# Low parts of split weights: an accumulating DMA in place of a vector subtraction, in a four-layer fp32 model

## The chip, the cores and the metric

One NeuronCore of a Trainium2 chip runs the whole program in one launch. The metric is the device time of one execution in microseconds (us), first instruction to last. Engines are named as the profile names them: PE (TensorE matmul), PEld (its weight loads), DVE (VectorE), ACT (ScalarE), POOL (GpSimd), SP (the sync engine, which only issues DMAs here). A small q behind a name (SPq) is the engine's own queue, where DMAs are issued.

## The reference, cut to what matters

Input x is 512 tokens by 1024 features, all in float32. Four mixing layers (L1: SSD and gated linear attention; L2: multi-head latent attention; L3: retention; L4: stick-breaking attention) each have a SwiGLU feed-forward layer behind them (F1 to F4, hidden width 2816):

```
for each layer:  x = x + mixer(rms_norm(x) * gain);  x = x + (silu(h @ w_gate) * (h @ w_up)) @ w_down
```

Nearly all of the arithmetic is products of activations with some 240 MB of weights, each weight used once per execution.

## The kernel before, in words

**Split operands.** Each float32 product is made of three passes on PE in the float32r type. An operand a is split into a high part (a rounded by a copy to float32r) and a low part (a minus the high part). A product is high·high + high·low + low·high, summed in PSUM: `mm3` (line 355) issues weights' high with the activations' high, weights' high with the activations' low, and weights' low with the activations' high. `mm3t` (line 454) does the same with the activations as the stationary operand; there the pass with the weights' low part is the second.

**Weight pieces.** The weights come in 455 pieces of at most 128 x 1024 float32 (512 KB), in the order of their use (`plan`, line 292). A piece passes through three steps. `wload` (line 330) has SP load it from DRAM to a tile `wr`. `wconv` (line 337) makes its high part `wh` with an ACT copy, and its low part `wl` with a DVE subtraction. `wpiece` (line 347) hands the two to the products. The tiles `wr`, `wh` and `wl` come from the pool `self.wp` with three buffers each, so a piece can be converted only when the piece three before it has had its last product. Helpers carry the line numbers of the profile: L221 is every ACT activation (`act`), L205 every two-operand vector operation (`tt`), L224 every matmul (`mm`), L334 the load of a piece.

```
def wconv(self):
    if self.raws:
        raw, ap = self.raws.popleft()
        n = ap.shape[-1]
        hi = self.wp.tile([128, 1024], F32R, tag="wh", name=self.nm("wh"))
        lo = self.wp.tile([128, 1024], F32R, tag="wl", name=self.nm("wl"))
        self.act(hi[:, :n], raw[:, :n], AF.Copy)
        self.tt(lo[:, :n], raw[:, :n], hi[:, :n].bitcast(F32), ALU.subtract)
        self.convs.append((hi, lo, ap))
...
def wpiece(self, ap):
    while len(self.convs) < 2 and self.raws:
        self.wconv()
        self.wload()
    hi, lo, at = self.convs.popleft()
```

**Who uses pieces.** Most pieces carry 8 stationary tiles of 128 x 128, used once each by `lin_a` (line 409) or `lin_b` (line 422): 24 passes a piece. In the feed-forward layers (`ffn`, line 471) 44 gate and up pieces are followed by 8 output tiles of the down projection, each of three pieces (1024, 1024 and 768 columns). `lin_bs` (line 436) differs: it takes all pieces of a block first, and then goes over the four token tiles, using each piece again in every one. In L2 (`mla`, line 930) a block of one 1024-column piece (keys and values) is followed by a block of two (768 and 384 columns, queries). In L4 (`sb`, line 1241) eight blocks have two 1024-column pieces each, so that two of the three buffers are in use for the whole block.

**Order.** The kernel is written as one sequence; the tile framework puts each engine's instructions in an order at compile time, from its own model of when each will be ready, and adds the semaphore waits. The order of an engine's instructions can so differ from the written one. In the mixing layers the steps of attention and of the scans run between the products as background work (`fill`, line 244, after each three-pass product). POOL has few instructions: sums of squares for the norms (L205), masks of layer 1 (L679), and some products. No DMA is issued from POOL. ACT reads PSUM and makes all exponentials, gates and high parts.

Of the kernel before, what the change touches and what calls it, by code (L numbers as in the profile page):

```python
# [9 lines left out]
F32 = mybir.dt.float32  # L10
# [7 lines left out]
EPS = 1e-6  # L18
# [148 lines left out]
class Emit:  # L167
# [15 lines left out]
        self.uid = 0  # L183
        self.ctx = ctx

# [1 line left out]
    def nm(self, s):  # L187
        self.uid += 1
        return f"{s}_{self.uid}"
# [52 lines left out]
        return True  # L242

    def fill(self):
        """called after each three-pass product: background steps at the set rate"""
        self.vn += 1
        if self.vq and self.vn % 2 == 0:
            self.vq.popleft()()
        if self.bg:
            self.credit += self.rate  # L250
            while self.credit >= 1.0:
                self.credit -= 1.0
                self.pump(1)
# [12 lines left out]
        self.pump(10 ** 9)  # L266

    def rsqrt(self, src, n, mul, out=None):
        """(src * mul + EPS) ** -0.5, elementwise on [128, n]"""
        v, i, a, y = self.S(n, "rv"), self.S(n, "ri", I32), self.S(n, "ra"), self.S(n, "ry")  # L270
        self.ts(v, src, mul, EPS, ALU.mult, ALU.add)
        self.ts(i, v.bitcast(I32), 1, None, ALU.logical_shift_right)
        self.ts(y.bitcast(I32), i, -1.0, float(0x5F3759DF), ALU.mult, ALU.add)
        for _ in range(3):
            self.stt(a, y, -0.5, y, ALU.mult, ALU.mult)
            self.mul(a, a, v)
            self.stt(y, a, 1.5, y, ALU.add, ALU.mult)
        return y

    def split(self, src, gain, name="h"):  # L280
        """src (SBUF or PSUM, times a per-partition gain) as float32r high and low parts"""
        n = src.shape[-1]
        hi, lo = self.T2(F32R, (128, n), name + "h"), self.T2(F32R, (128, n), name + "l")
        if gain is None:
            self.act(hi, src, AF.Copy)
            self.tt(lo, src, hi.bitcast(F32), ALU.subtract)
        else:
            self.act(hi, src, AF.Copy, scale=gain)
            self.stt(lo, src, gain, hi.bitcast(F32), ALU.mult, ALU.subtract)
        return hi, lo  # L290

    def plan(self, layers):
        """the weight pieces in the order of their use"""
        A = self.A
        for l in layers:
            if l[0] == "F":
                gu, wd = A[f"wgu{int(l[1]) - 1}"], A[f"wd{int(l[1]) - 1}"]
                for m in range(NFF):
                    yield gu[m, 0]
                    yield gu[m, 1]  # L300
                for m in range(8):
                    for c in (0, 1024, 2048):
                        yield wd[m][:, c:min(c + 1024, 2816)]
            elif l == "L1":
                yield from (A["w1a"][i] for i in range(12))
                yield from (A["w1b"][g, j] for g in range(2) for j in range(4))
                yield A["w1s"]
                yield from (A["w1a"][i] for i in range(12, 20))
                yield from (A["w1b"][g, j] for g in range(2, 6) for j in range(4))
                yield from (A["wo1"][i, m] for i in range(2) for m in range(8))  # L310
            elif l == "L2":
                yield from (A["wdq"][i] for i in (3, 4))
                yield A["wkr"]
                yield from (A["wdq"][i] for i in range(3))
                for g in range(4):
                    yield A["wukv"][g]
                    yield A["wuq"][g][:, 0:768]
                    yield A["wuq"][g][:, 768:1152]
                yield from (A["wo2"][i, m] for i in range(2) for m in range(4))
            elif l == "L3":  # L320
                for hd in range(4):
                    yield from (A["w3a"][4 * hd + i] for i in range(4))
                    yield from (A["w3b"][2 * hd + i, j] for i in range(2) for j in range(4))
                yield from (A["wo3"][i, m] for i in range(2) for m in range(8))
            elif l == "L4":
                yield from (A["w4b"][g, j] for g in range(2) for j in range(4))
                yield from (A["w4a"][g, s, j] for g in range(4) for s in range(2) for j in range(2))
                yield from (A["wo4"][i, m] for i in range(2) for m in range(4))
# [8 lines left out]
# [4 lines that stand above are left out]
            hi = self.wp.tile([128, 1024], F32R, tag="wh", name=self.nm("wh"))  # L341
            lo = self.wp.tile([128, 1024], F32R, tag="wl", name=self.nm("wl"))
            self.act(hi[:, :n], raw[:, :n], AF.Copy)
            self.tt(lo[:, :n], raw[:, :n], hi[:, :n].bitcast(F32), ALU.subtract)
            self.convs.append((hi, lo, ap))

    def wpiece(self, ap):
# [10 lines left out]
        self.mm(out, wl, xh, False, stop)  # L358
        self.fill()

# [1 line left out]
    def norm_prep(self, m, gain):  # L362
        self.h.append(self.split(self.x[:, m, :], self.col(gain, m)))
        self.norm_sq(m)
# [7 lines left out]
            self.add(self.acc, self.acc, sq, None if m == 7 else self.nc.gpsimd)  # L372

    def tok_sums(self, acc):
        """sums over the partitions of acc [128, 512], per token: [128 tok, 4]"""
        ps = self.MX()
        for t in range(4):
            self.mm(ps[:, t:t + 1], acc[:, t * 128:(t + 1) * 128], self.ones[:, 0:1])
        return ps

    def bcast_tok(self, r):
        """r [128 tok, 4] -> [128, 512], the tokens along the free axis on every partition"""
        ps = self.MX()
        for t in range(4):
            self.mm(ps[:, t * 128:(t + 1) * 128], r[:, t:t + 1].to_broadcast([128, 128]), self.ident)
# [2 lines left out]
        return o  # L388

    def norm_finish(self):  # L390
        """the row scales, rT and rbc, among the products that follow; row_scales() before their use"""
        def sums():
            ps = self.tok_sums(self.acc)
            self.rT = self.rsqrt(ps[:, 0:4], 4, 1.0 / 1024)
# [9 lines left out]
    def row_scales(self):  # L404
        if self.rbc is None:
            self.vflush()

# [1 line left out]
    def lin_a(self, pieces, hs, M=128):  # L409
        """pieces: [(ap [128, nk * M], nk)]; out [M, 512] features on partitions, in PSUM"""  # L410
        ps = self.LIN()
        K = sum(nk for _, nk in pieces)
        k = 0
# [6 lines left out]
        return ps  # L420

    def lin_b(self, pieces, hs, n=512):
        """pieces: [(ap [128, nk * n], nk)]; 4 x [128 tok, n] in PSUM"""
        pss = [self.LIN(), self.LIN(), self.LIN(), self.MX()]
        K = sum(nk for _, nk in pieces)
        k = 0
# [7 lines left out]
        return pss  # L434

    def lin_bs(self, pieces, hs, n):
        """as lin_b with the pieces all held: yields (t, [128 tok, n]) one after the other"""
        ws = []
        for ap, nk in pieces:
            wh, wl = self.wpiece(ap)  # L440
# [5 lines left out]
            yield t, ps  # L446

    def mm3s(self, out, w, x, n, start, stop):
        """a three-pass product of two split operands, n columns"""
        self.mm(out[:, 0:n], w[0], x[0][:, 0:n], start, False)  # L450
        self.mm(out[:, 0:n], w[0], x[1][:, 0:n], False, False)
        self.mm(out[:, 0:n], w[1], x[0][:, 0:n], False, stop)
# [14 lines left out]
                self.h = []  # L467
            self.norm_prep(m, gain)

# [1 line left out]
    def ffn(self, li, nxt):  # L471
        A = self.A
        self.norm_finish()
# [22 lines left out]
            self.residual(m, ps, gain)  # L496

    def out_two(self, w, hs, gain):
        """K = 512: a piece carries two output tiles"""
        for mp in range(4):  # L500
            wh, wl = self.wpiece(w[mp])
            for i in range(2):
# [3 lines left out]
                    self.mm3(ps, wh[:, s], wl[:, s], hs[k][0], hs[k][1], k == 0, k == 3)  # L506
                self.residual(2 * mp + i, ps, gain)

# [1 line left out]
    def ssd_gla(self, nxt):  # L510
        nc, A = self.nc, self.A
        self.norm_finish()
# [61 lines left out]
        self.out_a(A["wo1"][1], self.yh[8:16], nxt)  # L574

    def mix1(self):
        """the background steps of layer 1 in order"""
        def weave(main, side, at):
            n = 0
            for _ in main:  # L580
# [168 lines left out]
                yield  # L749

    def gla_gates(self):
        """cumulative log gates (times 16) of the four heads, restarting in each 64-token chunk"""
        nc = self.nc
        es, gs = [], []
        for hd in range(4):
# [106 lines left out]
            self.yh[8 + 2 * hd + i] = self.split(pt, self.col("glan", i))  # L862
            yield

# [1 line left out]
    def attention(self, nh, ready, prep, first, vcols, lag):  # L866
        """prep(hd): list of (lag, fn); first(hd, b): the weights of a 128-query block, st["p", b];
        vcols(hd, j): the values of the 128 keys of tile j, [128, 64]"""
        t, due, state = 0, [], {}
        todo = [(hd, b) for hd in range(nh) for b in range(4)]  # L870
        i = 0
# [31 lines left out]
            yield None if ran or due else "blocked"  # L903

    def weights_T(self, hd, j):
        """the weights of key tile j for the queries that see it, keys on partitions"""
        st = self.att[hd]
        pt = self.MX()
        for b in range(j, 4):
# [5 lines left out]
            self.act(wT[:, j * 128:], pt[:, j * 128:], AF.Copy)  # L915

    def pair_out(self, hp, vcols):
        """two heads' outputs, features on partitions, side by side in the array's columns"""
        po = self.MX()
        for j in range(4):  # L920
            for e in range(2):
# [4 lines left out]
            self.att.pop(2 * hp + e)  # L926
        self.oh[hp] = self.split(po, None)

# [1 line left out]
    def mla(self, nxt):  # L930
        nc, A = self.nc, self.A
        self.norm_finish()
# [22 lines left out]
        rk = self.rsqrt(self.tok_sums(acck)[:, 0:4], 4, 1.0 / 256)  # L955
        accq = down((0, 1, 2))
        cqh = [self.split(cf[i], self.col("qlora", i)) for i in range(3)]
        # rope tables with the gains in them, [128, 4, 32]
        self.ropec, self.ropes = self.S(128, "rc"), self.S(128, "rs")
        nc.sync.dma_start(out=self.ropec, in_=A["ropec"])  # L960
        nc.sync.dma_start(out=self.ropes, in_=A["ropes"])
# [42 lines left out]
                fn()  # L1004

    def mla_krope_a(self, kr):
        """the shared rotary part of the keys, under the heads' own parts in kT"""
        nc, tabs = self.nc, self.tabs
        pt = self.MX()
        for t in range(4):  # L1010
# [143 lines left out]
        hh, _, _, vs = self.heads[hd]  # L1154
        return vs[j][:, 64 * hh:64 * hh + 64]

# [1 line left out]
    def ret(self, nxt):  # L1158
        nc, A = self.nc, self.A
        self.norm_finish()  # L1160
# [76 lines left out]
            self.yh[4 * hd + i] = self.split(pt, self.col("retn", 4 * hd + i))  # L1237
            yield

# [1 line left out]
    def sb(self, nxt):  # L1241
        nc, A = self.nc, self.A
        self.norm_finish()
# [175 lines left out]
```

## Time and profile before

| | |
|---|---|
| time, two runs | 2818.6 and 2819.79 us, median 2819.19 |
| span of the profiled execution | 2818.6 us |
| PE, ACT, DVE, POOL busy | 99%, 36%, 52%, 5% of the span |
| DMA | 244.84 MB, 87 GB/s; SP's queue keeps the 16 DMA engines busy for 27.6% of the span |
| granted TensorE clock | 0.998 of 2.4 GHz over the span |

The span is the time from the first instruction to the last of one profiled execution, and the sums are made against it. A busy PE means that a matmul was in flight; matmuls overlap, so that a duration of 0.39 us and a start every 0.227 us go together. A row of the timeline gives the start in us, the duration in us, the engine, the line, the operation, its output and inputs, and in brackets the engine's idle time before it with what ended it.

### The profile page before, as it was taken

The numbers are of one execution on the slowest core, as the hardware profiler recorded it, in microseconds if no ns is written. First come the engines' busy times: TensorE is split into PE (matmuls) and PEld (weight loads), VectorE is DVE, ScalarE is ACT, GpSimd is POOL, SyncE is SP. The second block draws the span as 40 slices with busy tenths as digits, with TensorE's granted clock in tenths as the row PEclk, the third lists the DMA queues.
The fourth block names the chain that finished last, engine by engine and source line by source line (L and its number), as shares of the span: only waits on it lengthen the run. The fifth ranks groups of instructions, "written<-read, shape, count | busy, mean of one in ns | idle before, by whom it ended". The sixth has DMA issues, their size and how long they took to land.

```text
span 2818.6 us, 33289 instructions
## 1 busy us (share of the span) xinstructions
PE 2792.1 (99%) x13205; PEld 2259.5 (80%) x13205; DVE 1458.1 (52%) x2412; ACT 1020.0 (36%) x1629; POOL 152.2 (5%) x134
## 2 busy tenths in 40 slices
PE   8999999999998999999999999999999999999999
PEld 6787668888876678888888888888888987788887
DVE  7476564444349964443345554544433488744432
ACT  5444333332236652222233332332322365533321
POOL 1011001000012110000000000100000100100000
PEclk9999999999999999999999999999999999999999
DMA  4232212323321112333332222223333211133232
GB/s 155 85 106 93 72 53 92 98 95 98 96 78 40 46 60 97 97 97 90 115 96 85 77 87 82 90 97 98 96 96 97 87 53 45 53 96 98 93 105 80
DMA packets 72698, 244.84 MB, mean 87 GB/s; under 512 B 8208, under 2 KB 10064, under 8 KB 72544
## 3 DMA queue, kind: packets, MB, share of 16 engines
q1 hardware_dynamic: 72544, 242.72, 27.6%
q8 instruction: 104, 1.70, 0.2%
q14 instruction: 50, 0.41, 0.0%
HBM read 240.56 MB, written 2.13 MB: 86 GB/s over the span
## 4 chain that ended last, share of the span: by engine, by line
PE 94%; DVE 2%; issue 2%; ACT 1%; POOL 0%; DMA 0%; SPq 0%; POOLq 0%; ACTq 0%; DVEq 0%
PE lin L224 80%; PE mx L224 11%; PE mx L228 2%; POOL sq L205 0%; DVE wl L205 0%; DVE hl L214 0%; ACT wh L221 0%; DVE y L205 0%; ACT sq L221 0%; ACT hh L221 0%; DMA L<-acd 0%; DVE m L1143 0%; DVE e L769 0%; DMA x<-in_xT_dram 0%; DVE x L205 0%
## 5 line engine op out<-in xcount | busy, mean ns | idle before, releaser
L221 ACT ACTIVATE wh<-wr 128x1024 fp32r<-128x1024 f32 (+1 forms) x455 | 471.3, 1036 | 1279.5 <-PE lin L224 666.9
L224 PE MATMUL lin<-hh,wh 128*128 128x512 f32 (+1 forms) x2136 | 841.3, 394 | 7.6 <-ACT wh L221 7.5
L224 PE MATMUL lin<-hl,wh 128*128 128x512 f32 (+1 forms) x2136 | 835.9, 391 | 0.7 <-DVE hl L214 0.6
L224 PE MATMUL lin<-hh,wl 128*128 128x512 f32 (+1 forms) x2136 | 834.7, 391 | 0.8 <-DVE wl L205 0.8
L205 DVE TENSOR_TENSOR wl<-wr,wh 128x1024 fp32r<-128x1024 f32 (+1 forms) x455 | 545.7, 1200 | 477.6 <-ACT wh L221 477.1
L224 PEld LDWEIGHTS lin<-hh,wh 128*128 128x128 f32 (+1 forms) x2136 | 401.1, 188 | 98.3 <-issue 7.8
L224 PEld LDWEIGHTS lin<-hl,wh 128*128 128x128 f32 (+1 forms) x2136 | 401.4, 188 | 86.7 <-DVE hl L214 3.6
L224 PEld LDWEIGHTS lin<-hh,wl 128*128 128x128 f32 (+1 forms) x2136 | 401.1, 188 | 86.6 <-DVE wl L205 2.0
L224 PE MATMUL lin<-fh,wh 128*128 128x512 f32 x704 | 273.9, 389 | 0.0
L224 PE MATMUL lin<-fl,wh 128*128 128x512 f32 x704 | 273.9, 389 | 0.0
L224 PE MATMUL lin<-fh,wl 128*128 128x512 f32 x704 | 273.9, 389 | 0.0
L224 PE MATMUL lin<-wh,hh 128*128 128x512 f32 (+2 forms) x720 | 261.3, 363 | 0.8 <-ACT v L221 0.7
L224 PE MATMUL lin<-wh,hl 128*128 128x512 f32 (+2 forms) x720 | 252.3, 350 | 0.0
L224 PE MATMUL lin<-wl,hh 128*128 128x512 f32 (+2 forms) x720 | 251.7, 350 | 0.0
L205 DVE TENSOR_TENSOR u<-lin,bc 128x512 f32<-128x512 f32 x88 | 60.8, 691 | 282.5 <-PE lin L224 282.5
L205 POOL TENSOR_TENSOR sq<-sq,sq 128x512 f32<-128x512 f32 x51 | 76.1, 1492 | 1704.3 <-ACT sq L221 1690.4
L205 DVE TENSOR_TENSOR g<-lin,bc 128x512 f32<-128x512 f32 x88 | 60.8, 691 | 194.6 <-PE lin L224 185.7
L224 PEld LDWEIGHTS lin<-wh,hh 128*128 128x128 f32 x720 | 137.0, 190 | 24.2 <-issue 4.7
L224 PEld LDWEIGHTS lin<-fh,wh 128*128 128x128 f32 x704 | 132.2, 188 | 27.5
L224 PEld LDWEIGHTS lin<-fh,wl 128*128 128x128 f32 x704 | 132.2, 188 | 27.4
L224 PEld LDWEIGHTS lin<-fl,wh 128*128 128x128 f32 x704 | 132.2, 188 | 27.3
L224 PEld LDWEIGHTS lin<-wh,hl 128*128 128x128 f32 x720 | 136.5, 190 | 17.0 <-issue 0.6
(259 smaller groups left out, 2672.7 us busy)
## 6 DMA issues: line engine op xcount, KB each, us to landing
wr<-in_wgu_dram SPq DMA_DIRECT2D x176, 512.0 KB, 3.5
wr<-in_wd_dram SPq DMA_DIRECT2D x64, 512.0 KB, 3.5
wr<-in_wo_dram SPq DMA_DIRECT2D x48, 512.0 KB, 3.5
wr<-in_w3b_dram SPq DMA_DIRECT2D x32, 512.0 KB, 3.6
wr<-in_w1b_dram SPq DMA_DIRECT2D x24, 512.0 KB, 3.5
wr<-in_wd_dram SPq DMA_DIRECT2D x32, 384.0 KB, 3.2
wr<-in_w1a_dram SPq DMA_DIRECT2D x20, 512.0 KB, 3.6
wr<-in_w3a_dram SPq DMA_DIRECT2D x16, 512.0 KB, 3.6
```

The lines of the kernel that those rows point to most:

```text
L205: (eng or self.nc.vector).tensor_tensor(out=out, in0=a, in1=b, op=op)
L221: self.nc.scalar.activation(out, a, f, **k)
L224: self.last = self.nc.tensor.matmul(out, lhsT, rhs, start=start, stop=stop, **k)
L228: self.nc.tensor.transpose(out, in_, self.ident[0:n, 0:n])
```

## The change

The two lines that make a piece's parts become three. The high part is made as before. ACT then writes the negated high part into the low part's tile, and a DMA issued from POOL reads the raw weights from DRAM once more and adds them to that tile in SBUF. The other lines of the diff take comments and docstrings out.

```
@@ -341,7 +341,8 @@
             hi = self.wp.tile([128, 1024], F32R, tag="wh", name=self.nm("wh"))
             lo = self.wp.tile([128, 1024], F32R, tag="wl", name=self.nm("wl"))
             self.act(hi[:, :n], raw[:, :n], AF.Copy)
-            self.tt(lo[:, :n], raw[:, :n], hi[:, :n].bitcast(F32), ALU.subtract)
+            self.act(lo[:, :n], hi[:, :n].bitcast(F32), AF.Copy, scale=-1.0)
+            self.nc.gpsimd.dma_start(out=lo[:, :n], in_=ap, accum_op=ALU.add)
             self.convs.append((hi, lo, ap))
```

## Rows read from the trace of the kernel before

**Rows 1.** The page, part 1: busy time, share of the span, instructions.
```profile
PE 2792.1 (99%) x13205; PEld 2259.5 (80%) x13205; DVE 1458.1 (52%) x2412; ACT 1020.0 (36%) x1629; POOL 152.2 (5%) x134
```

**Rows 2.** The page, part 5: conversion of pieces (busy, mean ns | idle before).
```profile
L221 ACT ACTIVATE wh<-wr 128x1024 fp32r<-128x1024 f32 (+1 forms) x455 | 471.3, 1036 | 1279.5 <-PE lin L224 666.9
...
L205 DVE TENSOR_TENSOR wl<-wr,wh 128x1024 fp32r<-128x1024 f32 (+1 forms) x455 | 545.7, 1200 | 477.6 <-ACT wh L221 477.1
```

**Rows 3.** Timeline, ACT in F1's gate and up products.
```profile
504.97 1.06 ACT L221 ACTIVATE wh<-wr 128x1024 fp32r<-128x1024 f32 x1 [3.11 <-PE lin L224]
505.94 0.61 ACT L221 ACTIVATE g<-g 128x512 f32<-128x512 f32 x1
510.41 1.06 ACT L221 ACTIVATE wh<-wr 128x1024 fp32r<-128x1024 f32 x1 [3.86 <-issue]
```

**Rows 4.** Timeline, PE: first low pass of the piece converted at 504.97.
```profile
516.28 0.39 PE L224 MATMUL lin<-hh,wl 128*128 128x512 f32 x1
```

**Rows 5.** Timeline, ACT and PE in F1's down projection: conversion, first low pass.
```profile
704.89 1.06 ACT L221 ACTIVATE wh<-wr 128x1024 fp32r<-128x1024 f32 x1 [3.29 <-issue]
...
714.84 0.39 PE L224 MATMUL lin<-fh,wl 128*128 128x512 f32 x1
```

**Rows 6.** Timeline, L4: second pieces of blocks 1, 2 and 8, conversion and first low pass.
```profile
2207.07 1.06 ACT L221 ACTIVATE wh<-wr 128x1024 fp32r<-128x1024 f32 x1 [4.38 <-PE mx L224]
...
2213.86 0.28 PE L224 MATMUL lin<-wl,hh 128*128 128x256 f32 x1
...
2222.58 1.06 ACT L221 ACTIVATE wh<-wr 128x1024 fp32r<-128x1024 f32 x1 [0.97 <-PE lin L224]
...
2225.38 0.28 PE L224 MATMUL lin<-wl,hh 128*128 128x256 f32 x1
...
2339.67 1.06 ACT L221 ACTIVATE wh<-wr 128x1024 fp32r<-128x1024 f32 x1 [0.24 <-PE lin L224]
...
2345.89 0.28 PE L224 MATMUL lin<-wl,hh 128*128 128x256 f32 x1
```

**Rows 7.** Timeline, L2: two pieces with a short lead, conversion and first low pass.
```profile
848.43 1.06 ACT L221 ACTIVATE wh<-wr 128x1024 fp32r<-128x1024 f32 x1
...
853.50 0.85 ACT L221 ACTIVATE wh<-wr 128x768 fp32r<-128x768 f32 x1 [0.51 <-PE lin L224]
...
854.00 0.40 PE L224 MATMUL lin<-wl,hh 128*128 128x512 f32 x1
...
859.42 0.34 PE L224 MATMUL lin<-wl,hh 128*128 128x384 f32 x1
```

**Rows 8.** Timeline, the start: first conversion on ACT, and four rows of PE.
```profile
6.43 1.04 ACT L221 ACTIVATE wh<-wr 128x1024 fp32r<-128x1024 f32 x1
...
8.79 0.79 PE L224 MATMUL lin<-hh,wl 128*128 128x512 f32 x1
...
13.89 0.39 PE L224 MATMUL lin<-hh,wh 128*128 128x512 f32 x1
15.07 0.50 PE L224 MATMUL lin<-hh,wl 128*128 128x512 f32 x1 [0.80 <-DVE wl L205]
```

**Rows 9.** The page, part 6: loads of gate and up pieces, issue to landing.
```profile
wr<-in_wgu_dram SPq DMA_DIRECT2D x176, 512.0 KB, 3.5
```

**Rows 10.** Timeline, L4: one issue on SP's queue, one operation on POOL.
```profile
2224.57 1.22 POOL L205 TENSOR_TENSOR sq<-qk 128x512 f32<-128x512 f32 x1 [4.72 <-ACT qk L221]
...
2224.92 0.33 SPq L334 DMA_DIRECT2D wr<-in_w4a_dram  x1
```

**Rows 11.** DMA view of 500 to 690 us: packets, MB, share of 16 engines.
```profile
q1 hardware_dynamic: 5040, 18.09, 29.8%
```

**Rows 12.** Windows: 810 to 1053 us (PE, PEld, DVE, ACT, POOL busy; clock; DMA).
```profile
810.00:1053.00 243.00, 233.55 (x1251) 174.16 (x1249) 190.21 (x593) 139.78 (x330) 40.23 (x41) 0.99 0.16 50
```

**Rows 13.** Waits of the whole run: total us, times, longest us.
```profile
POOL L L679 <- DMA L<-acd: 151.9, 6, 135.7
...
PE mx L224 <- DVE sqk L205: 3.9, 1, 3.9
```

## The prediction before the run

> **What bounds the kernel now.** I read the page's busy shares first. PE is busy 2792.1 us of 2818.6, so 26.5 us at most is idle PE time, and DVE, from which the change takes work, is busy 52% [rows 1]. The table of groups comes next: 455 subtractions of 1.20 us on DVE, 455 copies of 1.04 us on ACT, and both engines idle before most of them [rows 2]. The subtraction is therefore work beside PE; what counts is only whether a piece's low part is there when PE comes to its first low pass.
>
> So the third view is the timeline, for each piece's lead: from the start of its conversion on ACT to its first low pass. In gate and up products conversions start every 5.44 us, one piece's 24 passes [rows 3], and the piece converted at 504.97 has its first low pass at 516.28 [rows 4]: a lead of 11.31 us. The conversion starts when the piece three before it gives up its buffer, two pieces ahead. In the down projection the lead is 9.95 us for two pieces of three, because one of the two ahead is short [rows 5]. Today's chain, copy and subtraction, takes some 2.3 us of it.
>
> Few leads are short. In L4 two pieces fill two of the three buffers for a whole block, and the next block's second piece waits for one: leads of 6.79, 2.80 and 6.22 us in blocks 1, 2 and 8 [rows 6]; the eight sum to 43.4 us (6.79, 2.80, 2.80, 5.62, 6.45, 6.22, 6.45, 6.22). In L2 two pieces have 5.57 and 5.92 us [rows 7]. The very first piece has 2.36 us [rows 8]. Elsewhere, a few at 7.7 to 9.7 us aside, leads are 9.95 us or more.
>
> **The change part by part.**
>
> Removed: 455 subtractions, 545.7 us of DVE. DVE paces little: the longest named wait of PE for it is 3.9 us, in L2 [rows 13], where PE idles 243.00 - 233.55 = 9.5 us in all [rows 12]. Gain between 0 and 9.5 us; I take 4, the row's own size. Added: 455 ACT copies. No SBUF to SBUF copy of this form has a row; the high part's is the nearest, 1.04 us, so ACT goes from 1020 to some 1490 us, 53%. In L2 ACT is at 139.8 of 243 us [rows 12], and 15 or so pieces there add under 16. This hides behind PE; uncovered it is 1.06 us a piece where PE waits for the low part, counted next. In gate and up products the gate's activation (0.61 us, rows 3) may come between the two copies; the lead still has room. `wr` is now free after the first copy, so SP's loads start earlier; they set nothing.
>
> Added too: 455 DMAs on POOL's queue, each 512 KB from DRAM added into SBUF. No row has one. Call D the time from the end of the second copy to the landing. Lower end: a plain load of the same size, 3.5 us [rows 9]. Upper end: three movements in sequence, the weights in, the old values read, the sum written, 3 x 3.5 = 10.5 us. My value has three terms. The plain load is 3.5. A second read keeps the DMA engines as long again as the first: 29.8% of 190 us for 18.09 MB is 34.5 pieces, 1.64 us each [rows 11]. POOL has to prepare the DMA; SP's issue takes 0.33 us and a POOL operation 1.22 [rows 10], and I take the upper, since POOL is new at this, 1.3. That is 6.4, and with some meeting of loads D = 6.5 us, nearer the plain load than the sequence.
>
> The chain from the start of the conversion is then 1.06 + 1.06 + 0.1 + 6.5 = 8.7 us, against the leads:
> - gate and up 11.31, down 9.95: nothing; it lies beside two pieces of products.
> - L4: 8 x 8.7 - 43.4 = 26.2 us of PE waiting, in eight stalls of 1.9 to 5.9 us.
> - L2: 8.7 - 5.57 = 3.1 us; the next piece's conversion started before that stall, which covers it.
> - Start: 8.7 - 2.36 = 6.3 us.
>
> Together 35.6 us. What is queued behind a waiting low pass is all of PE, so these count in full, unless PE has passes with the high parts to run meanwhile. Its order is set at compile time and can do that: at the start a high pass of the next tile, at 13.89, stands ahead of a low pass that had to wait until 15.07 [rows 8]. In a block of L4 eight high passes could go first; they have 256 columns, half of the others, whose starts are 5.44 / 24 = 0.227 us apart, so about 1 us of each stall. Between 0 and 8 us; I take 8.
>
> POOL's queue: the DMA waits there for ACT's second copy, and what stands behind it is norm sums with slack. The other way round, POOL waits 151.9 us in 6 waits for layer 1's decay rows [rows 13], and DMAs written behind these would be late; leads in layer 1 are mostly over 11 us, so I take nothing, and at worst a few us each.
>
> DMA engines: 1.64 us a piece now; with two reads 4.9 of 5.44 us, 90%. That holds, with little to spare; at the lower end it is 3.3, at three movements 6.6.
>
> Here the Trainium skill has the only price for an addition in a DMA: Collectives: The Full Stack, in "The bandwidth ceiling: the fold count and why AG ≠ RS ≠ AR", says that the adding itself costs nothing and the second source read halves the rate, with a measured ratio of 1.93. No row here shows it; by it a piece would take 3.2 us of the DMA engines, as in my value. Another page speaks for less: DMA: Bandwidth & Descriptors, "Anatomy of one DMA", fits 2.0 us plus bytes over 436 GB/s to a DMA of POOL's path, an estimate of 3.2 us here, which the plain load's 3.5 us nearly agrees with; if it held for an accumulating one, the chain would be 5.4 us and the sum some 8 us of stalls.
>
> Sum: 2818.6 + 35.6 - 8 - 4 = 2842 us, +0.8%. The median of the runs is 0.6 us above the span, so I forecast 2843.
>
> **The rivals.** About 2% is what a measurement of this kernel tells from no change.
>
> *The DMA engines become the bound (slower).* If an accumulating DMA holds an engine for more than 5.44 - 1.64 = 3.8 us a piece, transfers can't follow PE in the long product stretches. For it: I stand at 3.3, with 90% in use, and loads and additions share the engines. Against: 3.8 is 2.3 times a plain load. Price at three movements, 6.6 us a piece: a feed-forward layer of 44 x 5.44 + 8 x 14.96 = 359 us becomes 1.21 times as long, 4 x 75 = 300 us; the first 20 pieces of layer 1 and the output projections add some 40. About 3155 us.
>
> *The chain outgrows the ordinary leads (slower).* With D = 9 us, because POOL takes 3 us or more to prepare a DMA or the loads get in between, the chain is 11.2 us: L4 46 us, L2 6, start 9, and 1.25 us in each of 32 down-projection tiles, 40. Less the 12 taken above, about 2908. It decides from D of some 8 us on. For it: two engines' hand-overs and a queue of which the trace shows nothing. Against: gate and up would still be covered.
>
> *DVE's relief pays more than the stalls (a little faster).* With D = 3.5 us the chain is 5.7 us, stalls are 9.4 us (two of 2.9 us in L4, 3.3 at the start), and the idle time in L2 and in the scans of layer 1 gives up to 20 back: 2808. Against: PE's 26.5 idle us are all there is, 7.5 of them at the start where nothing can be gained. More than 2%, 56 us, could come only from passes that PE now starts late without being idle.
>
> **How the numbers follow.** Hidden with stalls in L4, L2 and at the start: 0.50, 2843 us (its own range 2825 to 2870, D from 5 to 8). DMA engines the bound: 0.18, 3155. Chain too long: 0.22, 2908. DVE's relief: 0.10, 2808, of which 0.02 beyond 2%. Slower by over 2% is 0.18 + 0.22 = 0.40; faster 0.02; within 2% 0.58. The range goes from 2806, just under the last rival, to 3160, just over the first; some 0.15 is left out, nearly all of it above, where an addition takes more than three movements.
>
> **What would show it.** Right: in gate and up products starts of conversions stay 5.44 us apart and PE has no gap; PE's waits name the new DMA only at the start, at 854 us in L2, and eight times in L4, 2 to 6 us each; DVE near 910 us, ACT near 1490; DMA share in the feed-forward layers near 0.9 and landing near 5 to 6 us after the issue on POOL. Wrong: regular gaps on PE once per piece, with conversions more than 5.44 us apart (the DMA bound: share at 1.0, landing times growing), or gaps only at the first two pieces of each down-projection tile (the chain); POOL busy above half of the span would say that preparing the DMAs is the cost.

## The result, and the profile after

The changed kernel takes 2864.86 us (median of 2 runs, 2862.54 to 2867.19) against 2819.19 before: ratio 1.0159, 95% interval 1.0142 to 1.0177. The forecast was 2843 us, slower within 2%; the change is slower by 1.6%, inside the range and on the forecast side, and 22 us above the number. The profiled execution took 2867.19 us with a span of 2865.4, so 46.8 us of span have to be found.

The page of the changed kernel, parts 1, 3, 5 and 6 (it answers to [rows 1, 2, 9]; L345 is the line of the new DMA):

```profile
PE 2806.0 (98%) x13205; PEld 2272.2 (79%) x13205; DVE 958.3 (33%) x1957; ACT 1457.9 (51%) x2084; POOL 530.4 (19%) x589
...
q0 software_dynamic: 65520, 231.83, 50.0%
q1 hardware_dynamic: 72544, 242.72, 26.0%
...
L221 ACT ACTIVATE wl<-wh 128x1024 fp32r<-128x1024 f32 (+1 forms) x455 | 469.3, 1031 | 9.2
...
L345 POOL DMA_DIRECT2D wl<-in_wgu_dram x176 | 152.1, 864 | 786.3 <-ACT wl L221 780.1
...
wr<-in_wgu_dram SPq DMA_DIRECT2D x176, 512.0 KB, 3.8
wl<-in_wgu_dram POOLq DMA_DIRECT2D x176, 512.0 KB, 6.1
```

DVE lost 500 us of work and PE gained nothing by it: DVE was beside PE. The new queue q0 keeps the 16 DMA engines busy for half of the span; per piece that is 0.50 x 2865.4 / 455 = 3.15 us.

The long stretches took the load as forecast. Windows of the feed-forward layers F1 and F2 (PE, PEld, DVE, ACT, POOL busy; granted clock; DMA share; GB/s), then the timeline of ACT in the stretch of [rows 3]:

```profile
500.00:690.00 190.00, 190.00 (x840) 157.39 (x839) 49.18 (x71) 90.74 (x105) 30.20 (x35) 1.00 0.89 193
1100.00:1400.00 300.00, 300.00 (x1325) 247.99 (x1323) 60.06 (x87) 141.63 (x163) 55.74 (x62) 1.00 0.88 192
```

```profile
506.68 1.06 ACT L221 ACTIVATE wh<-wr 128x1024 fp32r<-128x1024 f32 x1 [2.77 <-PE lin L224]
507.65 0.62 ACT L221 ACTIVATE g<-g 128x512 f32<-128x512 f32 x1
508.17 1.04 ACT L221 ACTIVATE wl<-wh 128x1024 fp32r<-128x1024 f32 x1
512.12 1.06 ACT L221 ACTIVATE wh<-wr 128x1024 fp32r<-128x1024 f32 x1 [2.91 <-PE lin L224]
```

PE is busy throughout both windows at a DMA share of 0.88 to 0.89, and conversions start 512.12 - 506.68 = 5.44 us apart, as before. Where PE waits instead is in its waits over the whole run (total us, times, longest):

```profile
PE lin L224 <- DMA wl<-in_w4a_dram: 22.4, 8, 5.1
PE lin L224 <- ACT wh L221: 10.9, 2, 7.9
PE lin L224 <- DMA wl<-in_w1a_dram: 4.8, 1, 4.8
PE lin L224 <- DMA wl<-in_wukv_dram: 3.7, 1, 3.7
PE mx L228 <- DVE ac L633: 3.0, 1, 3.0
PE mx L224 <- POOL xe L205: 2.1, 1, 2.1
```

The wait for `in_w4a` is the eight blocks of L4, `in_w1a` the start, `in_wukv` L2. To see what each place cost I took, for each piece, the time of its last pass on PE in a trace less the same time before, and from that the growth in each stage (us; spans differ by a few tenths more than the totals, for the start and end of the program):

```
kernel               start  L1,F1 L2   F2 to L4's values  L4 blocks  after   total
the change             6.2   6.7  -2.9        1.8            36.5     -1.8    46.5
e1  L4 seconds sub     5.6   6.7  -3.3        2.2            -0.2     -1.1     9.9
e9  plain DMA          4.0   0.5  -3.9        0.5            10.3     -3.0     8.4
e10 L4 firsts sub      5.8   3.9  -2.8        2.1            26.0     -1.3    33.7
e7  L4 by lin_b        6.5   8.3  -2.8        2.5            -0.4     -2.1    12.0
e8  four buffers       6.7   5.5  -1.1        0.4             0.2     -2.6     9.1
e12 47 pieces sub     -0.2   2.2  -1.1        2.9            -0.3     -2.4     1.1
```

Differences of up to some 2 us in such a row are the spread between executions: e6 below has layer 1's instructions in the same order as the kernel before and shows 2.0 us at the end of F1, most of it between 45 and 155 us, where its granted clock is 0.97 for 0.98.

L4 holds 36.5 of 46.5 us. Its second block on PE, against [rows 6]:

```profile
2245.64 0.28 PE L224 MATMUL lin<-wh,hh 128*128 128x256 f32 x1
2250.84 0.58 PE L224 MATMUL lin<-wl,hh 128*128 128x256 f32 x1 [4.93 <-DMA wl<-in_w4a_dram]
2251.22 0.41 PE L224 MATMUL lin<-wh,hl 128*128 128x256 f32 x1
2251.44 0.41 PE L224 MATMUL lin<-wh,hh 128*128 128x256 f32 x1
```

Its conversion began at 2240.20 and its DMA was issued at 2242.65 (ACT and POOL):

```profile
2240.20 1.06 ACT L221 ACTIVATE wh<-wr 128x1024 fp32r<-128x1024 f32 x1 [0.96 <-PE lin L224]
2241.29 1.06 ACT L221 ACTIVATE wl<-wh 128x1024 fp32r<-128x1024 f32 x1
2242.26 0.46 ACT L221 ACTIVATE qk<-lin,ry 128x256 f32<-128x256 f32 x1
2242.61 1.05 ACT L221 ACTIVATE wh<-wr 128x1024 fp32r<-128x1024 f32 x1
```

```profile
2242.65 0.88 POOL L345 DMA_DIRECT2D wl<-in_w4a_dram  x1 [5.18 <-ACT wl L221]
2243.25 1.35 POOL L205 TENSOR_TENSOR sq<-qk 128x512 f32<-128x512 f32 x1
2245.05 0.88 POOL L345 DMA_DIRECT2D wl<-in_w4a_dram  x1 [0.44 <-ACT wl L221]
```

So the chain here is 2250.84 - 2240.20 = 10.64 us, not 8.7, and a second accumulating DMA is issued 2.4 us behind the first. In the eight blocks it is 9.98, 10.64, 10.86, 9.02, 8.97, 8.82, 8.83 and 11.34 us, 78.5 in all; less the leads of before, 43.4 us, that is 35.1 us by which low parts came late. It is near the 36.5 us of the table, but not the same thing, as the next rows show.

After such a wait PE goes on slower: the passes that follow start 0.21 us apart, where those ahead of it, as in the kernel before, start 0.12 apart. Windows of PE from the first low pass of the second piece to the next block's conversion, after and before (busy and recorded matmuls; granted clock; DMA):

```profile
2250.84:2258.80 7.96, 7.96 (x50) 0.73 0.20 40
```

```profile
2225.38:2234.10 8.72, 8.72 (x75) 1.00 0.38 122
```

Before the wait PE had run passes of the next two token tiles ahead (the order chosen at compile time does that in blocks 2 and 3; in blocks 4 to 8 it puts a high pass and some products of the background work ahead), so fewer were left, 50 recorded rows for 75; but the granted clock of the stretch was 0.73 of 2.4 GHz, a good part of it at the lower of the two levels, 1.2 GHz, and only 0.76 us came of it.

What the eight blocks lost can be read from PE alone. Windows from the first pass of the blocks to the last, before and after (length, busy and recorded matmuls; granted clock; DMA):

```profile
2212.31:2366.49 154.18, 154.18 (x1140) 1.00 0.17 52
```

```profile
2224.07:2414.83 190.76, 168.35 (x1140) 0.91 0.40 86
```

The same 1140 matmuls are in both. PE is idle for 190.76 - 168.35 = 22.4 us, the named waits on `in_w4a`, and busy for 168.35 - 154.18 = 14.2 us longer, at a granted clock of 0.91 for 1.00. So 22.4 us are waiting and 14.2 us are passes at the lower clock. Of the 35.1 us of lateness the other 12.7 were filled with passes that the compiled order had put ahead of the late ones.

### The profile page after: what moved, and what is told of

It is laid out like the page before. It is cut to its first block, busy times and chain, and to the rows that moved or that the text cites. A ratio compares the mean times of both kernels' runs of the same rounds, so it can differ in the third digit from the quotient of the medians.

```text
span 2865.4 us, 34193 instructions
## 1 busy us (share of the span) xinstructions
PE 2806.0 (98%) x13205; PEld 2272.2 (79%) x13205; DVE 958.3 (33%) x1957; ACT 1457.9 (51%) x2084; POOL 530.4 (19%) x589
## 4 chain that ended last, share of the span: by engine, by line
PE 88%; issue 4%; DVE 3%; DMA 3%; ACT 1%; POOL 1%; SPq 0%; POOLq 0%; ACTq 0%; DVEq 0%
PE lin L224 76%; PE mx L224 10%; PE mx L228 2%; DMA wl<-in_w4a_dram 2%; POOL wl L345 0%; ACT wh L221 0%; ACT wl L221 0%; DMA wl<-in_w1a_dram 0%; DMA wl<-in_wd_dram 0%; DVE m L1144 0%; DVE q L205 0%; DVE ra L205 0%; DMA wl<-in_w3b_dram 0%; POOL sq L205 0%; DMA wr<-in_w1a_dram 0%
## 5 line engine op out<-in xcount | busy, mean ns | idle before, releaser
L221 ACT ACTIVATE wl<-wh 128x1024 fp32r<-128x1024 f32 (+1 forms) x455 | 469.3, 1031 | 9.2
L345 POOL DMA_DIRECT2D wl<-in_wgu_dram x176 | 152.1, 864 | 786.3 <-ACT wl L221 780.1
L224 PE MATMUL lin<-wl,hh 128*128 128x512 f32 (+2 forms) x720 | 258.9, 360 | 26.1 <-DMA wl<-in_w4a_dram 22.4
L205 DVE TENSOR_TENSOR x<-lin,x 128x512 f32<-128x512 f32 x96 | 66.2, 690 | 480.8 <-PE lin L224 480.6
L224 PEld LDWEIGHTS lin<-wl,hh 128*128 128x128 f32 x720 | 142.7, 198 | 44.5 <-DMA wl<-in_w4a_dram 24.0
L224 PEld LDWEIGHTS lin<-wh,hl 128*128 128x128 f32 x720 | 142.3, 198 | 17.0 <-issue 0.3
```

The lines of the kernel that those rows point to most:

```text
L205: (eng or self.nc.vector).tensor_tensor(out=out, in0=a, in1=b, op=op)
L221: self.nc.scalar.activation(out, a, f, **k)
L224: self.last = self.nc.tensor.matmul(out, lhsT, rhs, start=start, stop=stop, **k)
L345: self.nc.gpsimd.dma_start(out=lo[:, :n], in_=ap, accum_op=ALU.add)
```

## The experiments

The theory: the loss is the longer chain of a piece, at the few places where PE's lead is shorter than it. Rivals: a second ACT copy that isn't free; the second stream of transfers; POOL's queue; the low clock. The kernel before, shared by all runs, has a median of 2820.55 us over 21 runs (2818.2 to 2822.8).

**e1, the subtraction put back for the eight second pieces of L4** (diff against the changed kernel):

```
+            k = self.nconv = getattr(self, "nconv", -1) + 1
+            if k in (364, 366, 368, 370, 372, 374, 376, 378):
+                self.tt(lo[:, :n], raw[:, :n], hi[:, :n].bitcast(F32), ALU.subtract)
+            else:
                 ...
```

> The changed kernel, with the vector subtraction put back for 8 of the 455 pieces: the second piece of each block of L4. Theory (L4's loss is eight late low parts, and the lower granted clock that each stall of PE leaves behind): all of L4's 36.6 us goes, time about 2829 us (ratio 1.003 to 1.005), no wait of PE for these pieces, granted clock 1.00 all through L4. Rival (the clock in L4 falls for another reason, such as the added work of ACT, POOL and the DMA engines): only the 22.4 us of named waits go, about 2843 us, and the clock in L4 stays near 0.8 to 0.9.

2830.68 us (2826.76 to 2834.72), ratio 1.0032 (1.0021 to 1.0043). L4's blocks cost what they did before (-0.2 us) at a granted clock of 1.00 (2224 to 2380 us), and no wait on `in_w4a` is left. Eight pieces of 455 carry three quarters of the loss.

**e2, 88 passes of padding ahead of L4's late passes** (changed kernel, in `lin_bs`):

```
+                if n == 256 and t == 0 and k == 4:
+                    self.pads = getattr(self, "pads", [12, 20, 20, 6, 6, 4, 6, 14])
+                    po = self.mxp.tile([128, 512], F32, tag="mx", name=self.nm("pad"))
+                    for _ in range(self.pads.pop(0)):
+                        self.mm(po, hs[0][0][:, 0:128], hs[1][0])
```

> The changed kernel with 88 more matmuls of 512 columns, whose result nobody reads, put on PE just ahead of the passes that stall in L4 (12, 20, 20, 6, 6, 4, 6, 14 in the eight blocks; 0.227 us each at the full clock, 20 us in all). Theory (a stall costs its wait and then passes at the lower clock level): the added passes lie inside the waits and keep the clock at 1.00, so the time falls by 8 to 14 us, to some 2853 us, although work is added. Rival (the clock doesn't hang on the stall): the time stays or rises by up to 20 us, 2865 to 2885.

2866.67 us (2863.57 to 2869.26), ratio 1.016 (1.0145 to 1.0175): no gain. The named waits in L4 fell from 22.4 to 12.1 us and the granted clock was 1.00 in most of L4, 0.91 and 0.83 in the windows of 2240 to 2280, yet L4 grew by 37.6 us. The 88 passes take 88 x 0.227 = 20 us, twice the 10.3 us of waiting that went. PE is busy for 179.8 us in the blocks (1228 matmuls); less the 20 us of padding and the 154.18 us of before, 5.6 us are left as the cost of the lower clock, where the changed kernel pays 14.2. Waiting, clock and padding make 12.1 + 5.6 + 20 = 37.7 us. So the padding did buy back some 8.6 us of clock, but cost more than it saved. In this kernel PE's compiled order also no longer runs passes of later tiles ahead of the late one, so part of the difference may be the order.

**e3, the second ACT copy alone**, on the kernel before:

```
             self.act(hi[:, :n], raw[:, :n], AF.Copy)
+            self.act(lo[:, :n], hi[:, :n].bitcast(F32), AF.Copy, scale=-1.0)
             self.tt(lo[:, :n], raw[:, :n], hi[:, :n].bitcast(F32), ALU.subtract)
```

> The kernel before, with the change's second ACT copy alone: ACT writes the negated high part into the low part's tile, and the vector subtraction then writes the low part over it; no DMA from POOL. Theory (ACT's 470 us lie beside PE): within 4 us of the kernel before, 2817 to 2823, but L4's second pieces, with 0.48 us to spare, lose 0.6 us each, 5 us more. Rival (ACT is what costs at the start and in layer 1): the 6 us of the start and the 6 us of layer 1 both appear, 2830 or more.

2823.98 us (2822.62 to 2829.43), ratio 1.0016 (1.0007 to 1.0026). 455 more copies, and the subtraction later by one of them, cost 3.4 us (2.0 to 7.3 by the interval), just above the 2817 to 2823 us that I expected; the 5 us expected for L4 are 1.4 in the trace.

**e4 and e5, the DMA beside the subtraction.** Both keep the kernel before and add the accumulating DMA into tiles that nothing reads. Both give up three of the 69 operand tiles for room. In e4 two fixed tiles, filled once:

```
+            self.nc.gpsimd.dma_start(out=self.spare[k % 2][:, :n], in_=ap, accum_op=ALU.add)
```

> The kernel before, with the change's DMA alone: low parts still by vector subtraction, and beside each one POOL issues the accumulating DMA of the same piece into one of two spare tiles that nobody reads (three of the 69 work buffers are given up for them). Theory (only the low part's lateness costs): within 6 us of the kernel before, 2815 to 2825, DMA share 0.88 in the feed-forward layers with no gap of PE. Rival (traffic or POOL's queue costs by itself): layer 1's 6 us and part of the start's 6 us appear, 2828 or more.

3532.31 us (3528.43 to 3535.68), ratio 1.2522 (1.2501 to 1.2543): a miss, and an artefact of the edit. Nothing tied a DMA to its conversion. Page of e4, the slices of PE, POOL and DMA:

```profile
PE   8905677639998000269999999999999999999999
...
POOL 3223332232222223331100000000100001000000
...
DMA  9999999999999999961122333222222332112232
```

All 455 DMAs ran off in the first 18 slices, with the DMA engines full; POOL's queue is served in order, and the norm sums and scan steps written between these DMAs came when the queue came to them. For three of those slices PE hardly runs. One wait of PE for a norm's squares lasted 325 us. It shows what POOL's queue can cost, not what the change's costs. e5 ties each DMA by ACT's copy into a tile of a two-buffer pool:

```
+            sp = self.wp.tile([128, 1024], F32R, tag="sp", bufs=2, name=self.nm("sp"))
+            self.act(sp[:, :n], hi[:, :n].bitcast(F32), AF.Copy, scale=-1.0)
+            self.nc.gpsimd.dma_start(out=sp[:, :n], in_=ap, accum_op=ALU.add)
```

> The kernel before with its subtraction kept, and the change's second ACT copy and its accumulating DMA made beside it into a spare tile of two buffers that nothing reads. The copy holds each DMA to its conversion, which the run with untied spare DMAs did not. PE waits for no low part here; what is paid is ACT, POOL's queue and the DMA engines alone. My theory (the change's loss is the length of the chain at PE's short leads): 2820 to 2828 us, of which up to 6 are layer 1, where POOL's steps stand behind DMAs that wait for ACT. Rival, the loss is what the second stream of transfers or POOL's queue does to everything else: 2845 to 2865 us, as the change itself.

2840.28 us (2837.71 to 2843.36), ratio 1.0069 (1.0054 to 1.0085), between the two. From F2 to the end of L4's blocks it loses 1.6 us with all the traffic running (its own growth: start 8.7, L1 7.2, L2 5.7, then 1.6), so the traffic in itself takes nothing from the long products or from L4. The early losses have a wait of my own edit in them (timeline of ACT):

```profile
35.95 1.06 ACT L221 ACTIVATE sp<-wh 128x1024 fp32r<-128x1024 f32 x1 [2.33 <-DMA sp<-in_w1a_dram]
36.91 0.58 ACT L221 ACTIVATE bc<-mx 128x512 f32<-128x512 f32 x1
```

ACT waits for a spare buffer, and the copy of the norm's scales behind it makes PE wait 4.0 us. How much of L1 and L2 here is that and how much contention stays open.

**e6, the DMA for the last 15 pieces of L2 alone**, elsewhere the subtraction; the diff is e1's with another condition:

```
+            if k not in range(140, 155):
```

> The kernel before, with the change's conversion for the 15 last pieces of layer 2 alone (from the second key piece on), where the trace of the change showed a stall of 3.7 us and then 9 us gained. My theory (the DMA pays only where DVE's queue holds up PE, here): 2808 to 2816 us, some 5 to 9 us under the kernel before, ratio 0.996 to 0.998. Rival, those 9 us were only a debt of the stall before them and of the other order of the work, so nothing is gained: 2819 to 2824 us.

2821.86 us (2819.07 to 2823.38), ratio 1.0003 (0.9994 to 1.0012). My expectation failed. L2 grew by -2.2 us and other stages took it back: 3.0 us at F2's first norm, 2.0 up to the end of F1, where nothing had been changed. The 9 us that the changed kernel regained inside L2 were probably for the most part the 5.6 us it had lost just before.

**e7 and e8, longer leads.** e7 computes L4's blocks piece by piece, so that a block doesn't hold two buffers; e8 has four buffers (and 66 operand tiles for 69):

```
-                for t, ps in self.lin_bs([(A["w4a"][g, s, j], 4) for j in range(2)], h, 256):
+                for t, ps in enumerate(self.lin_b([(A["w4a"][g, s, j], 4) for j in range(2)], h, 256)):
```

```
-            hi = self.wp.tile([128, 1024], F32R, tag="wh", name=self.nm("wh"))
-            lo = self.wp.tile([128, 1024], F32R, tag="wl", name=self.nm("wl"))
+            hi = self.wp.tile([128, 1024], F32R, tag="wh", bufs=4, name=self.nm("wh"))
+            lo = self.wp.tile([128, 1024], F32R, tag="wl", bufs=4, name=self.nm("wl"))
```

> The changed kernel, with L4's query and key blocks computed piece by piece into four PSUM tiles, so that a block no longer holds two of the three buffers at a time and the second piece's lead grows by the first piece's products. My theory (the leads of 2.8 to 6.8 us in L4 cost 36 of the 45 us lost): the named waits of PE on the DMA into w4a's low parts go, and the time falls to 2828 to 2838 us. Rival, the L4 loss belongs to what the DMA does to the engines there, or the low granted clock has another cause than these waits: 2855 us or more.

> The changed kernel with four buffers instead of three for the high and low parts of the weights, so that every conversion may start a whole piece earlier (some 5.4 us of lead more); three operand tiles fewer to make room. My theory: the stalls of L4 (36 us) and of the second key piece in L2 (4 us) go, those of the start (6 us) and of layer 1's scans (6 us) stay; 2815 to 2830 us, so no slower than the kernel before by over 0.4%. Rival, the loss is not a matter of leads but of the engines or of POOL's queue: 2850 us or more.

e7: 2832.03 us (2829.43 to 2833.99), ratio 1.004 (1.0026 to 1.0054). e8: 2827.88 us (2824.03 to 2829.74), ratio 1.0025 (1.0015 to 1.0035). In both, L4's loss is gone with every DMA still in place (-0.4 and 0.2 us). All of PE's waits of over 2 us in e8:

```profile
PE lin L224 <- ACT wh L221: 10.6, 2, 7.6
PE lin L224 <- DMA wl<-in_w1a_dram: 5.4, 1, 5.4
PE mx L224 <- DVE sqk L205: 3.7, 1, 3.7
PE mx L228 <- DVE ac L633: 3.0, 1, 3.0
PE mx L224 <- POOL xe L205: 2.4, 1, 2.4
```

Neither `in_w4a` nor `in_wukv` is among them; the start and L1 are left. The leads decide, not the traffic.

**e9, the same DMA without the addition.** The DMA overwrites the negated high part with the raw weights, which leaves out the split:

```
-            self.nc.gpsimd.dma_start(out=lo[:, :n], in_=ap, accum_op=ALU.add)
+            self.nc.gpsimd.dma_start(out=lo[:, :n], in_=ap)
```

> The changed kernel with POOL's DMA as a plain load over the negated high part: same queue, same place, same waits, no addition and so no second read; the low part is then the raw weights themselves, which leaves the split of the weights out. The order of PE's passes is that of the changed kernel. If the second read is the part of the landing that my sum gave it (1.6 us of 6.5): landing after POOL's issue falls from 6.1 to some 4.5 us in the feed-forward layers, from 8.2 to under 6.5 us in L4's blocks 2 and 3, L4's loss from 36 to some 20 us, the start's from 6.2 to 4.6, and the time is 2842 to 2850 us. Rival, POOL's preparing and the hand-overs make most of the landing: it stays at 5.5 us or more in the feed-forward layers, and the time at 2858 us or more.

2831.52 us (2829.15 to 2834.35), ratio 1.0042 (1.0027 to 1.0058). Every engine has the instructions of the changed kernel in the same order, so the 33 us between the two are the addition and what follows from it, and the time is 10 us below the range I expected. Its page:

```profile
q0 software_dynamic: 65520, 231.83, 28.8%
...
L345 POOL DMA_DIRECT2D wl<-in_wgu_dram x176 | 93.4, 531 | 844.9 <-ACT wl L221 837.8
...
wl<-in_wgu_dram POOLq DMA_DIRECT2D x176, 512.0 KB, 4.4
```

The landing falls from 6.1 to 4.4 us, as the sum had it, the share of the engines from 50.0% of 2865.4 us to 28.8% of 2827.4, a ratio of 1.76 for the same bytes, and POOL's own part from 864 to 531 ns. L4 loses 10.3 us where I expected 20. PE in the eight blocks:

```profile
2213.43:2377.93 164.50, 157.92 (x1140) 0.98 0.32 99
```

The chains are 7.22, 8.65 and 9.10 us in blocks 1 to 3 and 7.3 to 7.7 in the others, 62.2 us in all; less the leads of before that is 18.9 us of lateness. PE waits for only 6.6 of them, in blocks 1 to 3, and the passes put ahead fill 12.3: in blocks 4 to 8 the chains are longer than the old leads, and still no pass waits. The lower clock adds 3.7 us. So the chain less the lead isn't the loss; it overstates it here by 8.6 us. L1, which I had not named, came back to 0.5 us.

**e10, the subtraction put back for the eight first pieces of L4's blocks**, so that a second piece's DMA has no other one 2.4 us behind it:

```
+            if k in range(363, 379, 2):
```

> The changed kernel with the subtraction put back for the eight first pieces of L4's blocks; the second pieces, whose low parts PE waits for, keep the DMA. PE's order of passes in L4 stays that of the changed kernel. My theory (L4's chain came out at 9 to 10.9 us and not 8.7, since two accumulating DMAs that start 2.4 us apart share the engines): the second pieces land some 6.1 to 6.6 us after the issue and not 8.2 to 8.4 in blocks 2 and 3; L4 loses 22 to 29 us and not 36; 2851 to 2859 us. Rival, the landing is what it is there for another reason (the raw loads, POOL's queue): landings stay at 8 us, 2862 to 2868 us.

2853.97 us (2852.68 to 2861.31), ratio 1.0124 (1.011 to 1.0138). The DMAs of the second pieces of blocks 2 and 3 land 6.1 and 5.8 us after the issue, for 8.2 and 8.4. The eight chains sum to 70.4 us; less 43.4 that is 27.0 us of lateness, 8 less than in the changed kernel, and L4 grew by 26.0. PE in the blocks:

```profile
2221.27:2401.51 180.24, 165.88 (x1140) 0.93 0.30 71
```

That is 14.4 us of waiting and 11.7 at the lower clock; the passes put ahead fill 12.6. PE's order in L4 is that of the changed kernel, so the order isn't what made the difference.

**e11 and e12, the subtraction for the pieces with short leads**: e11 for 13 (the first three, two in L2, the eight of L4), e12 for those and the first 37 (47 in all, since three are in both), so that no DMA stands in POOL's queue in L1's scans:

```
+            if k in (0, 1, 2, 138, 139, 364, 366, 368, 370, 372, 374, 376, 378):
```

```
+            if k <= 36 or k in (138, 139) or k in range(364, 379, 2):
```

> The changed kernel with the subtraction put back for the 13 pieces with short leads alone: the three first, two in L2, and the eight second ones of L4. My theory: only layer 1's scans are left as a loss (6 us), less some 2 to 4 us of relief in L2; 2820 to 2826 us. Rival, pieces with long leads lose a little each: 2830 us or more.

> As the kernel with 13 pieces put back, with the subtraction put back for the first 37 pieces too, so that no DMA stands in POOL's queue ahead of layer 1's scan steps: 46 pieces subtracted, 409 by DMA. My theory (layer 1's 6 us are POOL's steps behind DMAs that wait for ACT, and the order that follows from it): 2814 to 2821 us, no slower than the kernel before and at best 3 us faster by L2's relief, within what the runs tell apart. Rival, the 6 us are DVE's and ACT's other order of the work: 2822 to 2827 us.

e11: 2829.49 us (2826.01 to 2836.06), ratio 1.0032 (1.0023 to 1.0041), 3.5 us above what I expected: 3.5 us at the start, where PE waits 2.0 us for a norm's scale on DVE and more at the lower clock behind it, and single waits on `in_w3b` and `in_wd` of 1 to 2.3 us, which are leads that the landing of those pieces just exceeds. e12: 2822.22 us (2820.08 to 2824.45), ratio 1.0006 (0.9998 to 1.0015): no better than the kernel before with 408 of 455 low parts made by DMA (the 46 and 409 above are one off). Both came out above what I expected, e12 by 1.2 us and so within the rival's range, which the runs can't tell from mine; none of the versions that were run beats the kernel before.

## Why the prediction came out right

The mechanism was right: the DMA lies beside PE in the long products, and PE pays at the short leads. The size was not: the sum added 23.6 us and 46.5 were found. The stated range, 2806 to 3160 us, is wide and would have held much else, so the sum is the better test. Of the 22.9 us between them 18.3 are L4 and 6.7 layer 1, less some 2 us elsewhere. By its own steps:

- **DVE's relief, 4 us taken.** DVE gave up 500 us, L2 ran 2.9 us shorter in the changed kernel, little more than the spread, and e6, with the relief alone, gained nothing that can be measured. PE's wait for `sqk`, from which the 4 us were taken, is still 3.7 us in e8, which has no subtraction at all. No run shows this gain.
- **ACT's copies, nothing.** 1031 ns each, ACT at 51%; e3 puts all of them at 3.4 us (2.0 to 7.3).
- **D, 6.5 us.** From the end of the second copy POOL takes 0.3 us to start (2242.35 to 2242.65), and the landing is 6.1 us after that in gate and up pieces: 6.4. Of its three terms the second read is the one measured: e9 gives 1.7 us for 1.64. The rest, POOL's start and a plain landing of 4.4 us, makes 4.7, for 3.5 + 1.3 in the sum. D grows where transfers meet: 8.2 and 8.4 us after the issue in L4's blocks 2 and 3, 8.4 for the first piece. The fit of the Trainium skill's page DMA: Bandwidth & Descriptors, "Anatomy of one DMA", which gave an estimate of 3.2 us, is below both landings, 4.4 and 6.1.
- **DMA engines, 90%.** 0.88 to 0.89 in the windows; 3.15 us a piece, against 3.28 for two reads in [rows 11]. Here the Trainium skill (Collectives: The Full Stack, "The bandwidth ceiling: the fold count and why AG ≠ RS ≠ AR") says of a reduce-scatter between cores that the addition costs no cycles and its second read halves the rate, 1.93 measured: the trace agrees as far as 1.92 against SP's load of [rows 11] (3.15 / 1.64), and 1.76 against the same queue without addition.
- **The start, 6.3 us**: 6.2, by luck. ACT and PE in the changed kernel:

```profile
6.83 1.06 ACT L221 ACTIVATE wh<-wr 128x1024 fp32r<-128x1024 f32 x1 [0.36 <-DMA wr<-in_w1a_dram]
...
18.12 0.80 PE L224 MATMUL lin<-hh,wl 128*128 128x512 f32 x1 [4.80 <-DMA wl<-in_w1a_dram]
```

The chain is 11.29 us and not 8.7 (the DMA landed 8.4 us after its issue, among the first loads). PE ran passes with high parts meanwhile, which the sum had not counted here, and the two errors cancel.

- **L2, 3.1 us** for one stall: 3.7, with no second one, as forecast.
- **L4, 26.2 us of waiting less 8 for PE's order: 18.2 forecast, 36.5 found.** This is the term that was mis-sized. The chain is 9.8 us on average and not 8.7, so that the lateness is 35.1 us instead of 26.2. Most of that is blocks 2, 3 and 8, where the next piece is converted right behind and its DMA, issued 2.1 to 2.4 us after, shares the engines: landings of 7.4 to 8.4 us. In block 6 the raw load comes as close behind as in blocks 2 and 3 (1.0 us) but the next such DMA 2.8 us, and the landing is 5.6 us. e10, which takes the first pieces' DMAs away, has 27.0. The reordering came, and more of it than forecast: passes put ahead fill 12.7 us, for 8. That leaves 22.4 us of waiting for 18.2. The rest, 14.2 us, is a cost for which the sum has no term: PE at the lower clock around and behind the waits. The clock of the blocks is 0.91 in the changed kernel, 0.93 in e10 and 0.98 in e9, in the order of their waiting (22.4, 14.4 and 6.6 us), and 1.00 in e1, where nothing waits and most of the DMAs still run. In the changed kernel and e10 the loss is close to the chain less the lead (36.5 for 35.1, 26.0 for 27.0), but only because the clock took back about what the passes put ahead had filled; e9 shows the two apart (10.3 for 18.9).
- **POOL's queue, nothing taken.** L1 lost 6 us, most of it in its scans (PE idles 4.5 us more than before between 45 and 400 us). Timeline of POOL in the changed kernel and in e9 (same order):

```profile
176.37 0.63 POOL L680 TENSOR_SCALAR_AFFINE_SELECT L<-L 128x512 f32<-128x512 f32 x1 [2.81 <-DMA L<-acd]
178.70 0.89 POOL L680 TENSOR_SCALAR_AFFINE_SELECT L<-L 128x512 f32<-128x512 f32 x1 [1.70 <-DMA L<-acd]
183.72 0.88 POOL L345 DMA_DIRECT2D wl<-in_w1a_dram  x1 [4.13 <-ACT wl L221]
184.33 1.35 POOL L205 TENSOR_TENSOR xe<-xdt,te 128x512 f32<-128x512 f32 x1
```

```profile
173.00 0.64 POOL L680 TENSOR_SCALAR_AFFINE_SELECT L<-L 128x512 f32<-128x512 f32 x1 [2.32 <-DMA L<-acd]
174.53 0.63 POOL L680 TENSOR_SCALAR_AFFINE_SELECT L<-L 128x512 f32<-128x512 f32 x1 [0.89 <-DMA L<-acd]
179.29 0.60 POOL L345 DMA_DIRECT2D wl<-in_w1a_dram  x1 [4.13 <-ACT wl L221]
179.91 1.06 POOL L205 TENSOR_TENSOR xe<-xdt,te 128x512 f32<-128x512 f32 x1
```

The step `xe` stands behind a DMA that waits 4.13 us for ACT, in both: the queue's head makes it late. With the addition the decay rows land later too (2.81 and 1.70 us of waiting for 2.32 and 0.89), and PE waits 2.07 us for `xe` and 3.04 for `ac`; in e9 the wait for `ac` is 1.39 us and that for `xe` is gone. So the queue's order alone costs little (e9 has it and lost 0.5 us in L1). The addition brings the rest, by the later landing of the decay rows or by POOL's longer issue, and no run took these two apart. e12, with no DMA in L1's scans, has neither wait (0.6 us for `ac`, as before, and none for `xe`). The 2.2 us that its row still shows for L1 and F1 are within the spread: e6, with an unchanged layer 1, shows 1.8 there.

Of the rivals, the DMA engines had room at 0.9 and the chain in the down projection stayed under its lead: one wait of 0.2 us on `in_wd` in the changed kernel.

## What to carry to other kernels

Work taken off an engine that isn't the bound pays nothing, while the latency put in its place is paid wherever a buffer's lead is short: list every lead against the new chain, with the chain as it is when the next transfer follows close behind. The chain less the lead is how late the operand comes; subtract what the compiled order can put ahead, and add what the passes cost at the lower clock around the waits (here 35.1 - 12.7 + 14.2). Where a DMA of 6 us replaces an operation of 1 us, a longer lead (a fourth buffer, or a block that holds only one) is the first thing to try: here it left 0.3 to 0.4% of the 1.6%. A queue that issues DMAs in order holds up what is written behind them, so look at who shares it.

## What was not expected of the hardware

An accumulating DMA of 512 KB occupies POOL for 0.86 us where the same DMA without addition takes 0.53 us. And a wait of PE is not over when it ends: in L4 22.4 us of waits came with 14.2 us of longer passes, and the same passes with no waits ran at a granted clock of 1.00. In the second block, after 4.93 us of waiting the granted clock of the next 8 us was 0.73, while PE before that wait and in the kernel before ran at 1.00; the passes started 0.21 us apart for 0.12.
